# Five pairs of gate blocks in seven products instead of four: a hybrid attention block on one Trainium2 core

## The chip, the cores and the metric

The kernel runs on one core of a Trainium2 chip. The metric is the device time of one execution in microseconds (us): 1453.43 us is the median of three runs of the kernel before (1452.85 to 1456.15). The core has a matrix engine (PE, with its weight load PEld), a vector engine (DVE), a scalar engine (ACT), a general engine (POOL) and an engine (SP) that here does nothing but issue DMA transfers. Each engine works through its own queue in order and waits for the others by semaphores.

## The reference

One block of a streaming encoder on 1024 rows of width 1024, all in float32:

- `h = rms_norm(x)`, `proj = h @ w_in`. The last 2048 columns of `proj` go through a sigmoid and are the two gates, `gate_sb` and `gate_diff`. This document is about those 2048 columns; in blocks of 128 they are the sixteen gate blocks, 0 to 7 for the first gate and 8 to 15 for the second.
- stick-breaking attention, 8 heads of 64: strictly causal weights out of products of sigmoids
- differential attention, 4 heads of 2 x 64: the difference of two softmax maps with a position bias, then a norm per head
- `merged = gate_sb * (y_sb @ w_sb_out) + gate_diff * (y_diff @ w_diff_out)`, `x = x + rms_norm(merged @ w_o)`
- `u = relu(rms_norm(x) @ w_up) ** 2`, `x = x + rms_norm(u @ w_down)`

## The kernel before

**Precision.** A float32 factor is split into two parts that PE multiplies fast, `hi` (a cast by ACT) and `lo` (the rest, a subtraction by DVE). A product is three matmuls, hi x hi, hi x lo and lo x hi. A block of weights is loaded and split by `load_split` (L96 to L105).

**A gate block formed plainly.** `gate(b)` calls `project`: for each half of the 1024 rows of `h`, 8 slices of the depth times 3 matmuls of 128x512. That is 48 matmuls for a block. The result is copied out of the accumulator (L486) and stored to `gate_dram`; the sigmoid is taken when the merge reads it back.

**A pair of gate blocks in seven products.** A product of 2x2 blocks can be had from seven products instead of eight, if sums of the blocks are formed first. Here the four quarters of `h` (its depth and its rows halved) and the four quarters of two neighbouring gate blocks' weights are such blocks. One product of quarters (`product_h`, L541 to L550) is 4 x 3 = 12 matmuls, so a pair is 84 matmuls where two plain blocks are 96.

- `first_two(i)` forms two of the seven products, B11 and B21, for two pairs side by side. The first of them is kept in `p1_dram`, because it is needed again; the sum of both is a finished quarter of the gate.
- `last_products` forms the other five for all pairs, one pair after another. Before it can begin it takes four pages out of the SBUF slots with the tags `kh` and `kl`, loads the sums of `h` (`T1` to `T4`, formed in two earlier units by `form_sums`) and splits them (`split_sum`, L573 to L580).
- For each pair `pair_sums` (L590 to L596) loads both weight blocks and has POOL form four sums, and `split_pair` (L603, L604) splits them into `w24`, `w32` and `w1`. Then `start` runs the product with T2 (accumulator `g_b`), and the loop those with T3 and T4 (`g_d`) and T1 and B22 (`g_c`). Each product is followed by an addition on DVE (L631, L641, L645, L649, L653).

**The order of the work.** The attention runs in eight units: `u` = 0 to 3 for the stick-breaking heads, 4 to 7 for the differential heads. A unit's own steps alternate between PE (scores `z`, L273 and L274; transposes, L292; products with the values) and ACT, POOL and DVE. So each unit also has filler, work for PE that does not depend on the unit's chain: `fill(u)` first projects the next unit's queries, keys and values (`prepare(u + 1)`), then forms the gate blocks of `GATES[u]`, then, in unit 6, `first_two`, and in unit 7 `last_products`. `parts_of_fill(u)` counts the filler's parts, and the loop over the units hands them out in proportion to the work of the unit's steps (`while done * total < cost * size`). What is written is not the final order: a planner simulates the engines and gives each engine, at every point, the earliest written instruction that is ready. Later work, so also the next unit's filler, moves up into gaps where its slots and inputs allow.

Slots that matter below: two accumulators `acc`, two score banks `sc`, four slots `w` for split weights, two slots `raw` for loaded ones, four slots each for `kh`, `kl` and `qs` (two of a unit, two of the next), and a single slot for `bias`, which is loaded anew for each differential unit (L397) and patched by POOL (L400).

Before the change eight blocks are formed plainly, two each in units 0, 2, 4 and 7, and eight as four pairs:

```
PLAIN = 8
GATES = [range(0, 2), range(2, 2), range(2, 4), range(4, 4), range(4, 6), range(6, 6), range(6, 6), range(6, 8)]
```

Unit 6 has `first_two(0)` and `first_two(1)`; unit 7 has two plain blocks and then `last_products`.

After the units follow the merge (`half_mix`, L762), the output projection (L872) and the two MLP products (L994 and L1170), which the change does not touch.

Of the kernel before, what the change touches and what calls it, by code (L numbers as in the profile page):

```python
# [9 lines left out]
F32 = mybir.dt.float32  # L10
# [6 lines left out]
P = 128  # L17
# [4 lines left out]
HALF = 512  # L22
# [9 lines left out]
DFF = 4096  # L32
NF = DFF // P
ORDER = (3, 1, 2, 0)
PLAIN = 8
GATES = [range(0, 2), range(2, 2), range(2, 4), range(4, 4), range(4, 6), range(6, 6), range(6, 6), range(6, 8)]


SBQ, SBK, DFQ, DFK, GATE = 0, 4, 12, 16, 24
# [3 lines left out]
def hybrid_block_kernel(  # L43
# [23 lines left out]
    dram = ctx.enter_context(tc.tile_pool(name="dram", bufs=1, space=DRAM))  # L67
    ps = ctx.enter_context(tc.tile_pool(name="ps", bufs=1, space=PSUM))

    def acc_tile(name):  # L70
        return ps.tile([P, HALF], F32, tag="acc", name=name, bufs=2)
# [20 lines left out]
    def tmp_tile(name):  # L92
        return stream.tile([P, HALF], F32, tag="tmp", name=name, bufs=1)
# [45 lines left out]
        for name in ("A11", "A12", "A22", "S1", "S2", "S3", "S4")  # L139
    }  # L140
    t_dram = {name: [dram.tile([P, 2, HALF], F32, name=f"{name}_dram{q}") for q in range(2)] for name in ("T1", "T2", "T3", "T4")}
    p1_dram = dram.tile([4, P, HALF], F32, name="p1_dram")
    bias_dram = dram.tile([N_DIFF, NREL], F32, name="bias_dram")
    bias_rows = dram.tile([N_DIFF, P, NREL], F32, name="bias_rows")

# [9 lines left out]
    with ExitStack() as actx:  # L155
# [376 lines left out]
        def halves(w, i):  # L532
            return tuple(p[:, i * HALF:(i + 1) * HALF] for p in w)
# [20 lines left out]

        def first_two(i):

            bs = [PLAIN + 4 * i + 2 * e for e in range(2)]
            ws = [load_split(w_in[GATE + b], f"wa{b}") for b in bs]
            accs = [acc_tile(f"c11_{i}_{e}") for e in range(2)]
            for e in range(2):  # L560
                product_h(accs[e], halves(ws[e], 0), "B11")
                p1 = tmp_tile(f"p1_{i}_{e}")
                nc.scalar.copy(p1, accs[e])
                nc.sync.dma_start(out=p1_dram[2 * i + e], in_=p1)
                yield
            for e in range(2):
                product_h(accs[e], halves(ws[e], 1), "B21", first=False)
                gt = tmp_tile(f"gt_{bs[e]}_0")
                nc.any.tensor_copy(gt, accs[e])
                keep_gate(bs[e], 0, gt)  # L570
                yield
# [13 lines left out]
        def pair_sums(n):  # L585

            b = PLAIN + 2 * n
            f0, f1 = (stream.tile([P, S], F32, tag="raw", name=f"fw{n}_{i}") for i in range(2))
            for i, f in enumerate((f0, f1)):
                nc.sync.dma_start(out=f, in_=w_in[GATE + b + i])  # L590
            s1 = page_in["s1"][:, n % 2, :]
            a11, a12, a21, a22 = (f[:, i * HALF:(i + 1) * HALF] for f in (f0, f1) for i in range(2))
            nc.gpsimd.tensor_tensor(s1, a21, a22, op=ALU.add)
            nc.gpsimd.tensor_tensor(a21, a11, a21, op=ALU.subtract)
            nc.gpsimd.tensor_tensor(a11, s1, a11, op=ALU.subtract)
            nc.gpsimd.tensor_tensor(a12, a12, a11, op=ALU.subtract)  # L596
            return s1, f0, f1
# [11 lines left out]
        def last_products():  # L609

            for name, tag in (("v", "kh"), ("s1", "kh"), ("qu", "kl"), ("w1", "kl")):
                page_in[name] = pa.tile([P, 2, HALF], F32R if name == "w1" else F32, tag=tag, name=f"page_{name}", bufs=4)
            summed = pair_sums(0)
            for n in range(2):
                nc.sync.dma_start(out=page_in["v"][:, n, :], in_=p1_dram[n])
            split_sum("T2", sum_pages("T2"))
            t3_hi = pa.tile([P, 2, 2, HALF], F32R, tag="v", name="t3_hi", bufs=3)
            t3_lo = [pa.tile([P, 2, HALF], F32R, tag="qs", name=f"t3_lo{q}", bufs=4) for q in range(2)]
            split_sum("T3", [(t3_hi[:, q], t3_lo[q]) for q in range(2)])
            for name in ("T1", "T4"):  # L620
                split_sum(name, sum_pages(name))
            q, u21 = (page_in["qu"][:, e, :] for e in range(2))

            def start(n):
                nonlocal summed
                w1, w24, w32 = split_pair(n, *summed)
                summed = pair_sums(n + 1) if n < 3 else None
                b = acc_tile(f"g_b{n}")
                product_h(b, halves(w24, 0), "T2")
                v = page_in["v"][:, n % 2, :]  # L630
                nc.vector.tensor_tensor(v, b, v, op=ALU.add)  # L631
                return v, w1, w24, w32

            begun = start(0)
            yield
            for n in range(4):
                b0 = PLAIN + 2 * n
                v, w1, w24, w32 = begun
                d = acc_tile(f"g_d{n}")
                product_h(d, halves(w32, 0), "T3")  # L640
                nc.vector.tensor_tensor(q, d, v, op=ALU.add)  # L641
                yield
                c = acc_tile(f"g_c{n}")
                product_h(c, w1, "T1")
                nc.vector.tensor_tensor(q, c, q, op=ALU.add)  # L645
                keep_gate(b0 + 1, 1, q)
                yield
                product_h(d, halves(w32, 1), "T4", first=False)
                nc.vector.tensor_tensor(u21, d, v, op=ALU.add)  # L649
                keep_gate(b0 + 1, 0, u21)  # L650
                yield
                product_h(c, halves(w24, 1), "B22", first=False)
                nc.vector.tensor_tensor(v, c, v, op=ALU.add)  # L653
                keep_gate(b0, 1, v)
                if n < 2:
                    nc.sync.dma_start(out=v, in_=p1_dram[n + 2])
                yield
                if n < 3:
                    begun = start(n + 1)
                    yield  # L660

        n_units = N_SB + N_DIFF

        def fill(u):
            if u + 1 < n_units:
                yield from prepare(u + 1)
            for b in GATES[u]:
                yield from gate(b)
            if u == n_units - 2:
                for i in range(2):  # L670
                    yield from first_two(i)
            elif u == n_units - 1:
                yield from last_products()

        def parts_of_fill(u):
            n = 0 if u + 1 == n_units else 4 if u % 2 == 0 else 8
            return n + 2 * len(GATES[u]) + (0 if u < n_units - 2 else 8 if u == n_units - 2 else 20)


        xs = normalised(0)  # L680
# [283 lines left out]
    for t in range(NT):  # L964
# [19 lines left out]
        if t == 4:  # L984
            summed = sums(0, stream.tile([P, HALF], F32, tag="tmp", name="s1_0", bufs=1))
# [24 lines left out]
    for i in range(AHEAD // 2):  # L1010
        accs = [bank(BANKS[i % 2], f"c11_{2 * i + e}") for e in range(2)]
# [9 lines left out]
    summed = None  # L1021
# [215 lines left out]
    for left, other in zip(STORED, ("B11", "T1", "T2", "T4", "T3", "B22", "B21")):  # L1237
        accs = [bank(BANKS[t], f"d{left}_{t}") for t in range(4)]
# [63 lines left out]
```

## Time and profile before

| what | value |
|---|---|
| median of 3 runs | 1453.43 us |
| the profiled execution's own time | 1453.24 us |
| its span, first to last instruction | 1451.5 us |
| PE busy | 1425.8 us, 98% of the span |
| DVE, ACT, POOL busy | 1017.3, 751.4, 388.4 us |
| granted PE clock | 0.999 |

PE busy counts the time in which at least one matmul is under way; matmuls overlap, so it is not a sum of durations. A hole is a time in which PE has none. DVE, ACT and POOL times are sums of their instructions. The rows of the trace give for a group of instructions its engine, its source line, what it writes and reads, how often it runs, the total and the mean duration, and the idle time ahead of it with what ended that. In a table of stretches each engine has its busy time and, in brackets, its instruction count.

### The profile page before, as it was taken

Reading aid. Unit: us, or ns where it says so; the run is one execution under the profiler, and the core shown is the slowest. Engines: PE = TensorE matmul, PEld = TensorE weight load, DVE = VectorE, ACT = ScalarE, POOL = GpSimd, SP = SyncE. Lnnn points to the kernel's source line nnn. Section 1 sums busy time; section 2 is a strip of 40 time slices with the busy share of each in tenths; the row PEclk is TensorE's granted clock in tenths of the full one; section 3 lists DMA queues with packets and bytes.
Section 4 is the critical chain, followed back from the end, with each engine's and each line's share of the span. In section 5 each row is a group of like instructions: output and inputs, shape, how many; then the busy total and the mean of one; then the engine's idle time right before and its main releaser. Section 6 shows DMA issues by size and latency. Waiting matters only on the chain. (4 is left out here: it accounts for less than half of the span.)

```text
span 1451.5 us, 19994 instructions
## 1 busy us (share of the span) xinstructions
PE 1425.8 (98%) x7238; PEld 1209.1 (83%) x7238; DVE 1017.3 (70%) x1352; ACT 751.4 (52%) x1325; POOL 388.4 (27%) x377
## 2 busy tenths in 40 slices
PE   7999999999999999999999999999999999999997
PEld 6888998899889888788888878888888888888886
DVE  5477998788657777854755489766664669764783
ACT  6465665666656776444534465444444443534350
POOL 2012322234125002210002334333330357232611
PEclk9999999999999999999999999999999999999999
DMA  5432312222323247475657736544446785678681
GB/s 207 111 94 66 77 48 81 66 73 70 110 94 109 82 153 240 153 277 179 190 167 234 238 129 208 177 159 145 139 159 200 263 276 180 211 236 285 191 288 58
DMA packets 100283, 233.09 MB, mean 161 GB/s; under 512 B 9964, under 2 KB 25560, under 8 KB 100184
## 3 DMA queue, kind: packets, MB, share of 16 engines
q1 hardware_dynamic: 85784, 211.89, 46.2%
q10 hardware_dynamic: 14400, 19.93, 3.8%
q8 instruction: 57, 0.93, 0.3%
q14 instruction: 42, 0.34, 0.1%
HBM read 160.45 MB, written 65.29 MB: 156 GB/s over the span
## 5 line engine op out<-in xcount | busy, mean ns | idle before, releaser
L356 DVE TENSOR_TENSOR_SCAN rest<-rest 128x896 f32<-128x896 f32 (+3 forms) x64 | 88.1, 1385 | 16.4 <-POOL rest L351 15.6
L351 POOL TENSOR_SCALAR_AFFINE_SELECT rest<-rest 128x128 f32<-128x128 f32 x64 | 26.5, 414 | 242.4 <-ACT rest L347 242.4
L762 PE MATMUL mix<-y,wmix 128*128 128x512 f32 x384 | 88.2, 390 | 0.2 <-DMA y<-y_dram 0.2
L762 PEld LDWEIGHTS mix<-y,wmix 128*128 128x128 f32 x384 | 71.9, 188 | 15.4 <-DMA y<-y_dram 0.6
L824 DVE TENSOR_TENSOR lS_lo<-raw_S,lS_hi 128x1024 fp32r<-128x1024 f32 x32 | 53.9, 1683 | 40.1 <-ACT lS_hi L817 40.1
L1170 PE MATMUL dS<-rT_hi,lS_hi 128*128 128x512 f32 x192 | 74.7, 389 | 0.0
L1170 PE MATMUL dS<-rT_lo,lS_hi 128*128 128x512 f32 x192 | 74.7, 389 | 0.0
L1170 PE MATMUL dS<-rT_hi,lS_lo 128*128 128x512 f32 x192 | 74.7, 389 | 0.0
L817 ACT CAST lS_hi<-raw_S 128x1024 fp32r<-128x1024 f32 x32 | 33.6, 1051 | 74.5 <-DMA raw_S<-s_dramS 40.7
L419 ACT ACTIVATE s<-s,low 128x896 f32<-128x896 f32 (+7 forms) x64 | 49.7, 777 | 40.4 <-DVE low L414 40.0
L347 ACT ACTIVATE rest<-z 128x512 f32<-128x512 f32 (+2 forms) x96 | 48.1, 501 | 27.7 <-PE z L274 19.8
L299 DVE TENSOR_TENSOR wtl_sb<-tr_sb,wth_sb 128x512 fp32r<-128x512 f32 (+1 forms) x80 | 48.0, 628 | 8.5 <-ACT wth_sb L298 8.1
L298 ACT CAST wth_sb<-tr_sb 128x512 fp32r<-128x512 f32 (+1 forms) x80 | 41.2, 555 | 24.5 <-PE tr_sb L292 24.1
L351 POOL TENSOR_SCALAR_AFFINE_SELECT beta<-beta 128x128 f32<-128x128 f32 x64 | 52.2, 816 | 2.7 <-ACT beta L348 1.9
L414 DVE CUSTOM_DVE_ANT_0 s<-z,bias 128x512 f32<-128x512 f32 (+3 forms) x64 | 37.3, 586 | 21.1 <-PE z L274 14.9
L207 PE MATMUL acc_gate<-h,hi_gate 128*128 128x512 f32 x128 | 50.6, 396 | 0.0
L208 PE MATMUL acc_gate<-h,lo_gate 128*128 128x512 f32 x128 | 50.5, 394 | 0.0
L206 PE MATMUL acc_gate<-h,hi_gate 128*128 128x512 f32 x128 | 50.4, 394 | 0.0
L994 PE MATMUL c<-hB_lo,wa_hi 128*128 128x512 f32 x128 | 49.9, 390 | 0.0
L994 PE MATMUL c<-hB_hi,wa_hi 128*128 128x512 f32 x128 | 49.9, 390 | 0.0
L1170 PE MATMUL dA<-rB_hi,lA_hi 128*128 128x512 f32 x128 | 49.8, 389 | 0.0
L1170 PE MATMUL dA<-rB_lo,lA_hi 128*128 128x512 f32 x128 | 49.8, 389 | 0.0
(397 smaller groups left out, 4814.1 us busy)
## 6 DMA issues: line engine op xcount, KB each, us to landing
s_dramS<-us SPq DMA_DIRECT2D x64, 256.0 KB, 4.1
raw_S<-s_dramS SPq DMA_DIRECT2D x32, 512.0 KB, 4.1
s_dramA<-u ACTq DMA_DIRECT2D x48, 256.0 KB, 2.3
raw_A<-s_dramA SPq DMA_DIRECT2D x24, 512.0 KB, 4.3
y<-y_dram SPq DMA_DIRECT2D x16, 512.0 KB, 5.2
g<-gate_dram SPq DMA_DIRECT2D x16, 512.0 KB, 4.5
raw_up<-in_w_up_dram SPq DMA_DIRECT2D x16, 512.0 KB, 4.0
up<-in_w_up_dram SPq DMA_DIRECT2D x16, 512.0 KB, 4.0
```

The lines of the kernel that those rows point to most:

```text
L206: nc.tensor.matmul(acc, w_hi[:, ks], b_hi, start=(k == 0), stop=False)
L207: nc.tensor.matmul(acc, w_hi[:, ks], b_lo, start=False, stop=False)
L208: nc.tensor.matmul(acc, w_lo[:, ks], b_hi, start=False, stop=(k == NK - 1))
L299: nc.vector.tensor_tensor(lo[:, :n], tr[:, :n], f32(hi[:, :n]), op=ALU.subtract)
L347: nc.scalar.activation(rest[:, c0:c1], z, AF.Sigmoid, scale=-1.0)
L351: nc.gpsimd.affine_select(tl[:, dg], tl[:, dg], pattern=[[-1, P]], compare_op=ALU.is_gt, fill=fill, base=0, channel_multiplier=1,)
L356: nc.vector.tensor_tensor_scan(back, back, back, 1.0, op0=ALU.mult, op1=ALU.bypass)
L419: e = nc.scalar.activation(s[:, :nk], s[:, :nk], AF.Exp, bias=low, scale=-1.0, accum_out=sums[:, m:m + 1],)
L762: nc.tensor.matmul(accs[c], st, mv[:, cs], start=(first and k == 0), stop=(last and k == 3))
L824: nc.vector.tensor_tensor(lo, raw, f32(hi), op=ALU.subtract)
L994: nc.tensor.matmul(acc, st[:, ks], mv, start=(first and k == 0 and i == 0), stop=(k == 3 and i == 2), skip_group_check=True,)
L1170: nc.tensor.matmul(acc, st[:, e, ts], mv[:, e, :], start=(first and e == 0 and i == 0), stop=(last and e == 1 and i == 2))
```

## The change

Six blocks are formed plainly and ten as five pairs. The plain blocks stand in units 0, 2 (one each), 4 and 6 (two each), none in unit 7. All three calls of `first_two` are in unit 6, the third for a single pair. `last_products` runs over five pairs.

```diff
-PLAIN = 8
-GATES = [range(0, 2), range(2, 2), range(2, 4), range(4, 4), range(4, 6), range(6, 6), range(6, 6), range(6, 8)]
+PLAIN = 6
+PAIRS = (16 - PLAIN) // 2
+FIRST_TWO = (6, 6, 6)
+GATES = [range(0, 1), range(1, 1), range(1, 2), range(2, 2), range(2, 4), range(4, 4), range(4, 6), range(6, 6)]
...
-    p1_dram = dram.tile([4, P, HALF], F32, name="p1_dram")
+    p1_dram = dram.tile([PAIRS, P, HALF], F32, name="p1_dram")
...
         def first_two(i):
 
-            bs = [PLAIN + 4 * i + 2 * e for e in range(2)]
+            bs = [PLAIN + 2 * n for n in range(2 * i, min(2 * i + 2, PAIRS))]
             ws = [load_split(w_in[GATE + b], f"wa{b}") for b in bs]
-            accs = [acc_tile(f"c11_{i}_{e}") for e in range(2)]
-            for e in range(2):
+            accs = [acc_tile(f"c11_{i}_{e}") for e in range(len(bs))]
+            for e in range(len(bs)):
                 product_h(accs[e], halves(ws[e], 0), "B11")
                 p1 = tmp_tile(f"p1_{i}_{e}")
                 nc.scalar.copy(p1, accs[e])
                 nc.sync.dma_start(out=p1_dram[2 * i + e], in_=p1)
                 yield
-            for e in range(2):
+            for e in range(len(bs)):
                 product_h(accs[e], halves(ws[e], 1), "B21", first=False)
...
-                summed = pair_sums(n + 1) if n < 3 else None
+                summed = pair_sums(n + 1) if n < PAIRS - 1 else None
...
-            for n in range(4):
+            for n in range(PAIRS):
...
-                if n < 2:
+                if n < PAIRS - 2:
                     nc.sync.dma_start(out=v, in_=p1_dram[n + 2])
                 yield
-                if n < 3:
+                if n < PAIRS - 1:
                     begun = start(n + 1)
                     yield
...
             for b in GATES[u]:
                 yield from gate(b)
-            if u == n_units - 2:
-                for i in range(2):
+            for i, at in enumerate(FIRST_TWO):
+                if at == u:
                     yield from first_two(i)
-            elif u == n_units - 1:
+            if u == n_units - 1:
                 yield from last_products()
 
         def parts_of_fill(u):
             n = 0 if u + 1 == n_units else 4 if u % 2 == 0 else 8
-            return n + 2 * len(GATES[u]) + (0 if u < n_units - 2 else 8 if u == n_units - 2 else 20)
+            return n + 2 * len(GATES[u]) + 4 * FIRST_TWO.count(u) + (5 * PAIRS if u == n_units - 1 else 0)
```

## The prediction

> **What bounds the kernel now.** I read the page first, for the bound, then a table of stretches around the units that change, then the waits of PE in the one stretch where it has holes. The page:
>
> ```profile
> span 1451.5 us, 19994 instructions
> ```
>
> ```profile
> PE 1425.8 (98%) x7238; PEld 1209.1 (83%) x7238; DVE 1017.3 (70%) x1352; ACT 751.4 (52%) x1325; POOL 388.4 (27%) x377
> ...
> PEclk9999999999999999999999999999999999999999
> ```
>
> PE is covered for 98% of the span and its granted clock is full in every slice. "Busy" alone would not prove a bound, since matmuls overlap; the pace does. In the second MLP product, where nothing interrupts (the first fence below), 884 matmuls fill 200 us, 0.226 us each. The second fence has the stretches of units 0 to 3, then the end of unit 6 and unit 7 in pieces: the time of the two plain blocks (542:571), the first products of the pairs (571:600) and the rest.
>
> ```profile
> 1200.00:1400.00 200.00, 200.00 (x884) 165.58 (x884) 141.22 (x103) 85.98 (x102) 85.48 (x41) 1.00 0.72 232
> ```
>
> ```profile
> 66.00:142.00 76.00, 75.22 (x407) 64.49 (x406) 56.88 (x68) 43.14 (x90) 17.39 (x33) 1.00 0.37 101
> 142.00:209.00 67.00, 66.80 (x472) 62.01 (x470) 61.15 (x86) 45.07 (x105) 20.26 (x32) 1.00 0.23 59
> 209.00:283.00 74.00, 74.00 (x409) 63.97 (x408) 60.37 (x75) 43.61 (x91) 18.60 (x32) 1.00 0.26 77
> 283.00:351.00 68.00, 67.45 (x476) 62.61 (x475) 61.37 (x87) 46.59 (x105) 20.74 (x33) 1.00 0.23 60
> ...
> 542.00:571.00 29.00, 29.00 (x147) 24.55 (x146) 20.33 (x38) 17.70 (x37) 5.70 (x5) 1.00 0.77 251
> 571.00:600.00 29.00, 26.16 (x126) 21.01 (x125) 28.35 (x48) 20.93 (x36) 8.23 (x4) 1.00 0.47 150
> 600.00:647.00 47.00, 47.00 (x245) 39.93 (x244) 31.44 (x61) 20.95 (x43) 10.64 (x8) 1.00 0.67 225
> ```
>
> After the length come PE, PEld, DVE, ACT and POOL. Only one of these stretches has a hole worth naming: 571:600, where PE is covered 26.16 of 29 us (2.84 us of hole) and DVE is busy 28.35 of 29. There DVE sets the pace; everywhere else it is PE. What PE waited for in that stretch, longest first:
>
> ```profile
> PE z L273 <- DVE low L414: 1.0, 1, 1.0
> PE g_b L547 <- DVE page_qu L649: 0.9, 1, 0.9
> PE g_c L547 <- DVE page_qu L645: 0.6, 1, 0.6
> PE g_d L547 <- DVE T L580: 0.3, 1, 0.3
> ```
>
> All four end on DVE, 2.8 us together. So a matmul less is time won, unless the work that comes with it opens holes; unit 7 is where to look.
>
> **The change, part by part.** *Matmuls.* Before: 8 plain blocks x 48 + 4 pairs x 84 = 720. After: 6 x 48 + 5 x 84 = 708. Twelve less, at 0.226 us: **-2.7 us**, all on the bounding engine. By unit: units 0 and 2 lose 48 each (-10.9 us each); unit 6 gains 96 in plain blocks and 24 in the third call of `first_two` (+27.1 us); unit 7 loses 96 and gains 60 (-8.1 us).
>
> *Work beside PE.* Prices:
>
> ```profile
> L104 DVE TENSOR_TENSOR lo_gate<-raw_gate,hi_gate 128x1024 fp32r<-128x1024 f32 x8 | 9.8, 1231 | 0.5 <-ACT hi_gate L103 0.5
> L604 DVE TENSOR_TENSOR w_lo<-fw,w_hi 128x1024 fp32r<-128x1024 f32 x8 | 9.8, 1222 | 1.2 <-ACT w_hi L603 1.2
> L604 DVE TENSOR_TENSOR page_w<-page_s,page_w 128x512 fp32r<-128x512 f32 x4 | 4.3, 1072 | 3.1 <-ACT page_w L603 3.1
> L649 DVE TENSOR_TENSOR page_qu<-g_d,page_v 128x512 f32<-128x512 f32 x4 | 2.8, 689 | 4.1 <-PE g_d L547 4.1
> L603 ACT CAST w_hi<-fw 128x1024 fp32r<-128x1024 f32 x8 | 8.4, 1050 | 9.8 <-PE g_c L547 3.6 <-DMA gate_dram<-page_qu 3.5 <-issue 1.9
> L486 ACT COPY gt<-acc_gate 128x512 f32<-128x512 f32 x16 | 9.4, 588 | 4.9 <-PE acc_gate L208 2.6 <-issue 2.4
> L595 POOL TENSOR_TENSOR fw<-page_s,fw 128x512 f32<-128x512 f32 x4 | 6.4, 1610 | 0.3
> ```
>
> On DVE two plain blocks give back 2 x 1.23 = 2.5 us. A pair costs one split in `first_two` (1.23), two of `w24` and `w32` (2.44), one of `w1` (1.07) and five additions (3.45), 8.2 us: 5.7 us more. On ACT two plain blocks give back two casts and four copies (4.4 us); a pair costs three such casts, one of `w1` (taken as half, 0.5) and two copies, 4.8 us: nothing to speak of. POOL gets four more sums, about 6.4 us by L595. The DMA queue of SP gets one store and one load of `p1_dram` more and loads the two weight blocks once more. Cover: behind 571:600, DVE is busy 31.44 of 47 us and POOL 10.64, so a fifth round fits there at no cost. If the cover were gone, as in 571:600, it costs up to 5.7 us of DVE.
>
> *Units 0 to 3.* Without the one block, unit 0 is 76 - 10.9 = 65.1 us for DVE work of 56.88 - 1.2, a load of 86%; unit 2 is 63.1 us for 59.2, 94%. Units 1 and 3 already run at 91% and 90% with holes of 0.20 and 0.55 us. I take **+0.3 us**; between 0 (the planner finds the gaps) and 1.5 us (twice the holes of the odd units).
>
> *The start of unit 7.* Here the cover goes. The last scores of unit 6, the reload of the bias, the first POOL sums and their repetition in the next pair:
>
> ```profile
> 544.87 0.28 PE L273 MATMUL z<-kh_dfk,qs_dfq 128*128 128x256 f32 x1
> ...
> 548.29 1.03 SPq L397 DMA_DIRECT2D bias<-bias_rows  x1
> 550.66 1.29 POOL L593 TENSOR_TENSOR page_s<-fw 128x512 f32<-128x512 f32 x1 [63.24 <-DMA t_lo<-T_dram]
> ...
> 555.10 1.34 POOL L596 TENSOR_TENSOR fw<-fw 128x512 f32<-128x512 f32 x1
> ...
> 571.69 0.61 PE L547 MATMUL g_b<-T,w_hi 128*128 128x512 f32 x2
> ...
> 577.01 2.22 POOL L593 TENSOR_TENSOR page_s<-fw 128x512 f32<-128x512 f32 x1 [19.64 <-DVE low L414]
> ...
> 583.87 1.60 POOL L596 TENSOR_TENSOR fw<-fw 128x512 f32<-128x512 f32 x1
> ```
>
> And the four transfers of the bias, from issue to landing:
>
> ```profile
> DMA to landing us min/median/max: 5.6/8.2/8.8
> ```
>
> The pages of `last_products` need the `kh` and `kl` slots of unit 6, so its chain begins with that unit's last score: four sums on POOL (550.66 to 556.44: 5.8 us; the second pair's took 577.01 to 585.47: 8.5), a cast (1.05) and a split (1.22), then `g_b`. That is 8.1 to 10.8 us. Unit 7's own scores wait as long, because the single bias slot is reloaded first: 5.6 to 8.8 us. Before, two plain blocks that need neither fill this time:
>
> ```profile
> 542.00:571.00 29.00, 24.23 (x95) 17.18 (x95) 1.74 (x3) 1.00 0.77 251
> ```
>
> This row is the 542:571 stretch for the plain blocks' accumulator alone: 95 of PE's 147 matmuls there, 95 x 0.226 = 21.5 of 29 us. The other 52 (unit 6's last transposes and products, unit 7's first scores) took 7.5 us. After the change only these are left against a chain of 8.1 to 10.8, and `parts_of_fill` sharpens it: it counts 4 + 4 + 12 = 20 parts for unit 6, but the third `first_two` yields 2, not 4, so 18 exist and they are all handed out before unit 6's last step. A chain of 8.1 to 10.8 us against 7.5 us leaves 0.6 to 3.3 us, and the 7.5 us are themselves a chain over ACT and DVE. I take **+2.5 us** of hole; at the low end 0, if the planner runs unit 6's last scores in earlier gaps so that the chain starts sooner; at the high end 8.1, if all of that PE work has run before the chain begins.
>
> The Trainium skill, "SBUF — State Buffer", section "Who interferes with whom", says a DVE instruction with two SBUF inputs and a POOL instruction that reads SBUF lock each other out for a whole instruction. The rows agree: 1.29 us for L593 when DVE was half idle, 2.22 when it was full. By that rule the long chain of 10.8 us would hold whenever DVE is splitting at that time, and the sum would be 0.8 us higher, at a hole of 3.3 us.
>
> *The holes of 571:600.* DVE was full there because the splits of T1 to T4 (L580) fell together with the first two pairs' splits and unit 7's first softmax:
>
> ```profile
> L580 DVE TENSOR_TENSOR T<-T,T 128x1024 fp32r<-128x1024 f32 x6 | 8.3, 1389 | 0.2 <-ACT T L577 0.2
> L580 DVE TENSOR_TENSOR t_lo<-t_lo,t_hi 128x1024 fp32r<-128x1024 f32 x2 | 2.4, 1222 | 0.2 <-ACT t_hi L577 0.2
> ```
>
> Eight splits, 10.7 us. Their slots are the pages of `h` that plain blocks and `first_two` read; these now finish in unit 6, so the splits can run in the boundary's waiting time or, for T2, earlier. I take **-1.0 us** of the 2.84; between -2.8 (all gone) and +2 (a third of the 5.7 us that DVE gains in work).
>
> *Sum*, against the profiled execution's 1453.24 us (span 1451.5 plus 1.7 around it): -2.7 + 0.3 + 2.5 - 1.0 = -0.9, so 1452.3. The median of the runs is 0.2 above the profiled one, so **1452.5 us**.
>
> **The rivals.**
> - *All cover stays* (faster). Unit 6's last scores run early, the boundary closes, and the T splits clear out of 571:600: -2.7 - 2.8 = -5.5, 1447.9 us; with holes as before it is -2.7, 1450.7. For it: the planner left just 2.84 us of hole in 60 us of unit 7. Against it: in the kernel before every unit still had filler when the next began.
> - *The start of unit 7 runs dry* (slower). One mechanism, the chain from unit 6's last score to `g_b` with no filler: at the full 8.1 us hole the sum is -2.7 + 0.3 + 8.1 - 1.0 = +4.7, 1458.1 us. It decides from a hole of 5.6 us on (5.6 - 2.7 = 2.9). For it: both ways forward, sums and bias, wait for the same last score. Against it: 7.5 us of PE work is there to fill.
> - *DVE becomes the bound of unit 7* (slower): if 28.35 of 29 goes on through the unit, the added 5.7 us all show, -2.7 + 5.7 = +3.0, 1456.4 us. Against it: 31.44 of 47 us.
> - *A slower pace after the hole* (slower): in this trace the granted clock is 1.00 in every stretch. If a hole of 8.1 us let it fall to half for one product, twelve matmuls would take 2.7 us more, 1460.8 us. The Trainium skill, "TensorE: Matmul & The Clock Gate", Part 1, says that an idle window of about 3.4 us does halve the clock; no hole in these stretches is that long, so no row here tests it.
>
> **How the numbers follow.** A measurement of this kernel tells about 0.2%, 2.9 us, from no change. The forecast, within 2.9 us of before (1450.5 to 1456.3), has 0.50; all cover staying, as far as it goes beyond 2.9 us, 0.28; the dry start 0.13; DVE as the bound 0.06; the slower pace 0.03. So faster 0.28, same 0.50, slower 0.22. The likeliest case's own range is 1450.5 to 1456.3. For 8 in 10 it reaches down to 1447.5 (no holes at all) and up to 1458 (the dry start at its full price).
>
> **What would show it.** The PE count falls by 12. In units 0 and 2 the distance from first score to first score shrinks by about 11 us with no new waits on DVE. Right for the boundary: one or two holes of 0.6 to 3.3 us in all between unit 6's last score and the first `g_b`, released by DVE's split (L604) or the scores' DVE. Right for the T splits: L580 before the first `g_b`, and fewer than 2.8 us of waits in the 29 us behind it. The forecast is wrong if holes at the boundary sum to under 0.5 or over 5.6 us, if waits of PE on DVE appear in units 1 to 3, or if holes turn up where the change does nothing, in the merge or the MLP.

## The result, and the profile after

The kernel after takes **1467.14 us** (median of five runs, 1464.84 to 1469.30) against 1453.43: a ratio of 1.0086, 95% interval 1.0074 to 1.0098. By that ratio it is slower by 12.5 us (0.0086 x 1453.4; the two medians are 13.7 us apart), where 1452.5 was forecast and 1458 was the upper end of the range. The profiled execution took 1464.84 us.

The page of the kernel after, its span and busy times:

```profile
span 1463.1 us, 20015 instructions
...
PE 1428.4 (98%) x7226; PEld 1209.6 (83%) x7226; DVE 1027.2 (70%) x1359; ACT 755.0 (52%) x1325; POOL 388.2 (27%) x381
```

PE has the 12 matmuls less that were counted, and is "98%" as before. Where the time was lost the page does not show; it has to be found by stage. The distances below run from the first scores (or the first matmul of a stage) to the next such matmul, in the two profiled executions; the third column is the matmuls that a stage gained or lost, at 0.226 us.

| stage | before | after | matmuls alone | beyond them |
|---|---|---|---|---|
| units 0 to 3 | 284.8 | 269.4 | -21.7 | **+6.3** |
| units 4 and 5 | 135.0 | 134.7 | 0 | -0.3 |
| units 6 and 7 | 160.5 | 184.3 | +19.0 | **+4.8** |
| merge | 88.7 | 88.3 | 0 | -0.4 |
| output projection | 92.5 | 95.5 | 0 | **+3.0** |
| from the up product to the end | 623.5 | 624.3 | 0 | +0.8 |

The last column sums to 14.2; less 2.7 it is, but for rounding, the 11.6 us between the two spans. Three places lost time.

**Units 0 to 3.** The stretches of the kernel after, each one unit long (length, then PE, PEld, DVE, ACT, POOL with counts, clock, DMA):

```profile
66.00:133.00 67.00, 66.50 (x362) 56.98 (x360) 51.87 (x60) 40.51 (x85) 15.86 (x29) 1.00 0.35 98
133.00:202.00 69.00, 66.14 (x470) 61.30 (x471) 64.02 (x94) 45.84 (x108) 19.97 (x36) 1.00 0.21 58
202.00:269.00 67.00, 65.50 (x364) 56.54 (x363) 57.15 (x70) 41.54 (x87) 16.05 (x30) 1.00 0.28 76
269.00:336.00 67.00, 66.02 (x472) 61.16 (x471) 63.11 (x94) 46.74 (x107) 18.82 (x35) 1.00 0.21 52
```

Units 0 and 2 became shorter, but unit 1 has a hole of 2.86 us (69.00 - 66.14) where it had 0.20, units 2 and 3 of 1.5 and 1.0. What PE waited for between 66 and 352 us, kernel after (total, times, longest):

```profile
PE av L328 <- DVE wtl_sb L301: 2.6, 3, 1.5
PE z L275 <- ACT beta L350: 1.6, 3, 1.0
PE acc_sbv L256 <- DVE kl_sbk L238: 0.8, 1, 0.8
PE acc_sbk L208 <- DVE qs_sbq L223: 0.5, 1, 0.5
PE acc_sbv L257 <- DVE lo_sbv L106: 0.3, 1, 0.3
```

and the same list of the kernel before:

```profile
PE acc_sbk L206 <- DVE qs_sbq L221: 0.8, 1, 0.8
PE av L326 <- DVE wtl_sb L299: 0.4, 1, 0.4
```

5.8 us for 1.2. DVE is busy 64.02 of 69.00 and 63.11 of 67.00 us in units 1 and 3, 93 and 94%, where it had 91 and 90. PE's longest waits are for DVE's splits of the unit's own attention weights (`wtl_sb`). The waits are not the whole loss: PE's holes grew from 1.5 to 5.8 us, 4.3 of the 6.3; the other 2 us are in time in which PE counts as covered.

**The boundary of units 6 and 7.** The timeline of the kernel after, PE's rows (start, duration; in brackets the idle time before and what ended it):

```profile
550.87 0.28 PE L276 MATMUL z<-kl_dfk,qs_dfq 128*128 128x256 f32 x1
554.32 1.54 PE L294 MATMUL tr_df<-ident,s 128*128 128x128 f32 x6 [3.18 <-DVE s L434]
555.52 1.20 PE L549 MATMUL c<-h,hi_wa 128*128 128x512 f32 x2
...
560.20 0.39 PE L549 MATMUL c<-h,lo_wa 128*128 128x512 f32 x1
```

DVE and POOL at that time:

```profile
551.23 1.10 DVE L390 SCALAR_TENSOR_TENSOR sq<-sq,r 128x512 f32<-128x512 f32 x1
552.25 2.01 DVE L434 SCALAR_TENSOR_TENSOR s<-s,sums,s 128x768 f32<-128x768 f32 x1
...
551.86 1.59 POOL L596 TENSOR_TENSOR fw<-fw,fw 128x512 f32<-128x512 f32 x1
```

and the same time cut into stretches of 3.41 us, the last figure but two being the granted clock:

```profile
549.74:553.16 3.42, 1.30 (x8) 0.86 (x6) 2.83 (x5) 2.00 (x6) 2.57 (x2) 1.00 0.87 283
553.16:556.57 3.41, 2.25 (x9) 2.06 (x10) 3.41 (x4) 2.80 (x5) 3.25 (x3) 0.50 0.89 320
556.57:559.98 3.41, 3.41 (x10) 2.65 (x9) 3.41 (x6) 3.12 (x6) 0.53 (x1) 0.50 0.81 304
559.98:563.40 3.42, 3.42 (x23) 2.87 (x22) 3.42 (x7) 3.42 (x7) 0.00 (x0) 1.00 0.67 208
```

There is one hole of 3.2 us (3.3 with a gap of 0.1 just ahead of it), and behind it the clock is 0.50 for 6.83 us: the third row has ten matmuls where 3.41 / 0.226 = 15 would fit. The twelve matmuls of the third `first_two`'s second product take 0.41 us each. An estimate: at half clock 2.25 + 3.41 us of matmuls are up to 2.8 us longer than they need be (the twelve alone are 2.2), so the hole costs nearly twice its length. Later unit 7 is better than before: its holes sum to 1.0 us, where they were 2.8.

Two ways forward were shut at once. The transposes wait for DVE's `s`. The twelve matmuls wait for ACT's copy of the product before them, and on ACT that copy stands behind a cast of `T` that waits for its load:

```profile
553.08 1.04 ACT L579 CAST T<-T 128x1024 fp32r<-128x1024 f32 x1 [1.39 <-DMA T<-T_dram]
554.03 0.61 ACT L605 CAST page_w<-page_s 128x512 fp32r<-128x512 f32 x1
554.55 0.58 ACT L565 COPY p<-c 128x512 f32<-128x512 f32 x1
```

**The output projection.** One of ACT's mean squares there, what PE waited for, and what ACT waited for on that store, all between 735 and 840 us of the kernel after:

```profile
794.81 0.60 ACT L111 ACTIVATE or<-o 128x512 f32<-128x512 f32 x1 [3.32 <-DMA x_dram<-xr]
```

```profile
PE trh L900 <- ACT ht L906: 2.2, 1, 2.2
...
ACT or L111 <- DMA x_dram<-xr: 7.7, 2, 4.4
```

and the last of these in the kernel before:

```profile
ACT or L109 <- DMA x_dram<-xr: 2.7, 1, 2.7
```

One row tile of `o` gets an SBUF slot out of which a row of `x` is still being stored; the mean square waits for that store, ACT's copies (`ht`) are queued behind it, and PE's next transposes wait for these.

### The profile page after: what moved, and what is told of

Same layout as the page of the kernel before. It is cut to its first block, busy times and chain, and to the rows that moved or that the text cites. A ratio compares the mean times of both kernels' runs of the same rounds, so it can differ in the third digit from the quotient of the medians.

```text
span 1463.1 us, 20015 instructions
## 1 busy us (share of the span) xinstructions
PE 1428.4 (98%) x7226; PEld 1209.6 (83%) x7226; DVE 1027.2 (70%) x1359; ACT 755.0 (52%) x1325; POOL 388.2 (27%) x381
## 5 line engine op out<-in xcount | busy, mean ns | idle before, releaser
L826 DVE TENSOR_TENSOR lA_lo<-raw_A,lA_hi 128x1024 fp32r<-128x1024 f32 x24 | 36.0, 1500 | 20.0 <-ACT lA_hi L819 18.5
L1172 PE MATMUL dA<-rB_hi,lA_lo 128*128 128x512 f32 x128 | 49.8, 389 | 0.0
L996 PE MATMUL c<-hB_hi,wa_lo 128*128 128x512 f32 x128 | 49.7, 389 | 0.0
L359 DVE TENSOR_TENSOR beta<-beta,rest 128x895 f32<-128x895 f32 (+3 forms) x64 | 48.2, 758 | 1.9
```

What stands on the lines that cost most here:

```text
L359: nc.vector.tensor_tensor(beta[:, :nk - 1], beta[:, :nk - 1], rest[:, 1:nk], op=ALU.mult)
L826: nc.vector.tensor_tensor(lo, raw, f32(hi), op=ALU.subtract)
L996: nc.tensor.matmul(acc, st[:, ks], mv, start=(first and k == 0 and i == 0), stop=(k == 3 and i == 2), skip_group_check=True,)
L1172: nc.tensor.matmul(acc, st[:, e, ts], mv[:, e, :], start=(first and e == 0 and i == 0), stop=(last and e == 1 and i == 2))
```

## The experiments

The first theory took up the first two of these readings: **A**, the plain blocks of units 0 to 3 were cover for a DVE that has no time left; **B**, the plain blocks of unit 7 were cover for the chain from unit 6 to the first sums; and the change removed both kinds. All times below are medians; a ratio is against the kernel before on the same chip in the same stretch of runs (its medians were 1454.7 to 1455.5 there). "The gates" are the number of plain blocks per unit; after, it is 1, 0, 1, 0, 2, 0, 2, 0, and `FIRST_TWO = (6, 6, 6)`.

### e1 and e2: one half of the change each

e1 is the kernel after with the plain blocks of units 0 to 3 left where they were, so that unit 6 loses its two:

```
-GATES: 1, 0, 1, 0, 2, 0, 2, 0
+GATES: 2, 0, 2, 0, 2, 0, 0, 0
```

> Five pairs as in the changed kernel, but the six plain blocks stand two each in units 0, 2 and 4, none in unit 6; first_two stays three times in unit 6. Theory A (units 0 to 3 became bound by DVE when units 0 and 2 lost a block each, which cost 6.5 us against the matmuls taken out): units 0 to 3 go back to 284.8 us as before, the holes of the boundary of units 6 and 7 stay, total about 1460.6 us. Theory B (the whole loss comes from the boundary of units 6 and 7, where cover is missing): unit 6 has two blocks of cover less still, so no gain, 1467 us or more.

e2 is the kernel before, four pairs, with only its plain blocks moved:

```
-GATES: 2, 0, 2, 0, 2, 0, 0, 2
+GATES: 1, 0, 1, 0, 2, 0, 2, 2
```

> Four pairs and eight plain blocks as before; alone the move of one block each out of units 0 and 2 into unit 6 is made (plain blocks 1, 0, 1, 0, 2, 0, 2, 2). No matmul less, unit 7 keeps its two plain blocks. Theory A: about +6.5 us over before, 1460 us, with PE waiting for DVE and ACT in units 1 to 3. Theory B: nothing lost there, 1453.4 us within 2 us.

e1: 1462.86 us, ratio 1.0053 (1.0035 to 1.0070). Units 0 to 3 take 284.5 us, so A's loss is gone; but units 6 and 7 take 167.0 where their matmuls and the old holes give 157.8, with a hole of 5.0 us and 10.2 us at half clock. e2: 1463.98 us, ratio 1.0060 (1.0043 to 1.0077): moving two blocks, without one matmul more or less, costs 8.5 us, and no hole opens between units 6 and 7. In its profile units 0 to 3 are 8.3 us over what their matmuls give; 6.8 us at half clock are part of that. The two halves are separate losses; each alone is more than the 2.7 us that the twelve matmuls are worth.

### e3 and e4: the third `first_two` elsewhere

```
-FIRST_TWO = (6, 6, 6)
+FIRST_TWO = (6, 6, 4)
```

e3 does this to the kernel after, e4 to e1.

> The changed kernel with the third call of first_two, the one for a single pair, in unit 4 instead of last in unit 6. Theory C (the 3.3 us hole at the end of unit 6 is the chain product, copy, product of the single pair, whose copy waits for the one slot tmp): that hole goes, about 1463.8 us. Theory B (it is missing cover): 24 matmuls less of cover in unit 6, hole as long or longer, 1467 us or more.

> Both: plain blocks two each in units 0, 2 and 4, the single pair's first_two in unit 4. Theories A and C together: 1467.1 - 6.5 - 3.3 = 1457.3 us; 1454 us if the 3.3 us that the changed kernel also lost behind the attention (a hole in the output projection) go too. Theory B: unit 6 has the least filler of all, the boundary opens to 5 us or more, 1462 us or more.

e3: 1471.06 us, ratio 1.0100 (1.0079 to 1.0122); e4: 1466.86, 1.0079 (1.0062 to 1.0097). With the call in unit 4, e4 is 4.0 us slower than e1, on the same chip. e3 is not clearly slower than the kernel after (their ratios differ by 2.0 us and their intervals overlap), and not faster by either figure. The boundary has holes of 2.1, 0.8 and 1.8 us (e3), with half clock for 10.2 and 13.7 us. So it is not the third call's place in unit 6 that opens the boundary.

### e5: the two blocks back in unit 7

The kernel after with its blocks placed anew: two each in units 0 and 2 as before the change, one in unit 4, and one in unit 7, before `last_products`:

```
-GATES: 1, 0, 1, 0, 2, 0, 2, 0
+GATES: 2, 0, 2, 0, 1, 0, 0, 1
```

> Five pairs, plain blocks 2, 0, 2, 0, 1, 0, 0, 1 over units 0 to 7: units 0 and 2 keep both blocks, the two blocks that the fifth pair replaces come out of unit 4 and out of unit 7, which keeps one as cover. first_two three times in unit 6. Theory A+B (the 14 us are units 0 to 3 that cannot be shortened, and a boundary of units 6 and 7 without cover): both causes are gone, the 12 matmuls show, 1450.7 to 1453 us where before is 1453.4. Theory D (any block taken out of an attention unit shows only about 7.5 of its 10.9 us, unit 4 too): 1454 to 1457 us.

1467.15 us, ratio 1.0083 (1.0059 to 1.0108). Units 4 and 5 take 133.9 us where 48 matmuls less should give 124.1: a block taken out of unit 4 gains 1.1 us of its 10.9, in a profile with 6.8 us at half clock there. In e8 below, with the same blocks and no half clock there, the two units take 131.3, a gain of 3.7. PE's longest waits in 335 to 475 us are of the same kind as in units 0 to 3, now in the differential heads:

```profile
PE av_d L371 <- DVE wtl_df L301: 1.7, 1, 1.7
PE acc_dfv L257 <- DVE lo_dfv L106: 1.0, 1, 1.0
PE z L275 <- DVE low L416: 0.6, 1, 0.6
```

But DVE, third after the length, had room in unit 4, the first of these two stretches:

```profile
351.00:426.00 75.00, 71.99 (x362) 60.40 (x361) 47.98 (x107) 41.13 (x81) 21.56 (x25) 0.95 0.35 104
426.00:485.00 59.00, 56.98 (x384) 51.46 (x383) 45.80 (x107) 38.96 (x85) 24.51 (x23) 1.00 0.32 92
```

So a block can be cover where DVE is busy 64% of the time. PE's longest wait there ends at 416.88 us, on DVE work that comes in a bunch: DVE had stood idle for 2.6 us, until 410.56, and was then busy almost without a pause. There is no slack in unit 4 to pay for unit 7's cover. At the boundary the one block in unit 7 did help in this run: no hole there is over 0.5 us.

### e6: is it DVE's throughput?

The kernel after with 14 of DVE's splits in units 0 to 3 left out: for these weights (two gate blocks, queries, keys and values) `hi` is used in place of `lo`. The low part of these products is therefore left out of the result. The edit also takes no `w` slot for these `lo` parts, so it frees slots as well as DVE time.

```
         nc.scalar.copy(hi, raw)
+        if name in RELIEVED:
+            return hi, hi
         nc.vector.tensor_tensor(lo, raw, f32(hi), op=ALU.subtract)
```

> The changed kernel without 14 of DVE's weight splits (1.22 us each, 17 us) that run in units 0 to 3; the matmuls use the hi part in place of the lo part there, so their number and order of dependence on the attention stay, and the lo part of these weights is left out of the result. Theory A (DVE's throughput bounds units 1 to 3): PE's 5.8 us of waits in 66 to 352 us shrink to about the 1.2 us of before, 1462 us. Rival (the waits are the chain's latency over ACT, POOL and DVE, which has too little PE filler beside it): waits and time stay, 1467 us.

1461.64 us, ratio 1.0047 (1.0032 to 1.0062): 5.5 us less than the kernel after. Units 0 to 3 take 265.6 us for 269.4, and PE's waits there fall from 5.8 to 3.0 us:

```profile
PE av L331 <- DVE wtl_sb L304: 2.1, 5, 0.9
PE z L278 <- ACT beta L353: 0.7, 2, 0.3
PE acc_dfk L211 <- DVE qs_dfq L226: 0.2, 1, 0.2
```

PE's holes there fall from 5.8 to 3.3 us, so the work that was left out has a part in them. But the time was not won. Units 4 and 5 take 137.5 us for 134.7, units 6 and 7 185.5 for 184.3: from the first scores to the merge both kernels take 588.5 us. Eight matmuls less fall into units 0 to 3, eleven more into units 4 and 5, and PE waits there instead, between 332 and 472 us of e6:

```profile
PE acc_dfv L260 <- DVE lo_dfv L109: 1.1, 1, 1.1
PE tr_df L297 <- DVE s L437: 0.8, 1, 0.8
PE av_d L373 <- ACT wth_df L303: 0.3, 1, 0.3
```

The boundary's hole stayed at 3.2 us. What e6 is shorter by in its profile lies behind the units: the output projection takes 92.5 us for 95.5, and the merge is 0.5 shorter. So A is not shown: DVE's splits take part in the waits of units 0 to 3, but whether DVE's load or the length of the units' chains sets the loss stays open, as e5 does for unit 4.

### e7 and e8: POOL's sums earlier

Two pages of `last_products` are taken from a free slot of the values' kind, and `T3`'s `hi` pages go to `kh` in exchange, so that POOL need not wait for unit 6's `kh`; e7 on the kernel after, e8 on e5.

```
-for name, tag in (("v", "kh"), ("s1", "kh"), ("qu", "kl"), ("w1", "kl")):
+sv = pa.tile([P, 2, 2, HALF], F32, tag="v", name="page_sv", bufs=3)
+page_in["s1"], page_in["v"] = sv[:, 0], sv[:, 1]
...
```

> The changed kernel with the pages for the first sums and p1 in the third slot v, which is free in unit 6, and T3's hi pages in kh in exchange: POOL can form the first pair's sums before unit 6's last score. Theory E (the 3.3 us hole at the end of unit 6 is DVE held up by POOL's sums: its instructions of 0.7 to 1.2 us take 1.7 to 2.3 there): the hole shrinks to under 1 us, 1464 us. Theory B (missing cover): PE has no more to do than before, the hole stays or moves, 1467 us.

> Both e5 and e7. If the boundary in e5 still has a hole from POOL's sums, it closes: 1450 to 1451 us, faster than before by about 3 us. If the cover of one plain block already closes it: as e5 within 1 us.

1466.50 us, ratio 1.0088 (1.0066 to 1.0110), and 1466.42, 1.0079 (1.0055 to 1.0103): no difference to the versions without it. In e7 POOL's first sum started at 550.75 us, as before the edit (550.51), now held by the load of its weights. The edit did not move what it was to move, so e7 says nothing on the theory; e14 asks the question in another way. In e8 the sums did move, from 552.83 us (e5) to 545.61. The boundary did not close: a hole of 3.1 us opened, this time ahead of unit 7's scores, and no half clock followed it:

```profile
555.14 0.50 PE L275 MATMUL z<-kh_dfk,qs_dfq 128*128 128x512 f32 x1 [3.08 <-DVE low L416]
```

### e9 and e10: cover for the boundary

e9 is e1 with the third `first_two` in unit 7, ahead of `last_products`. e10 is the kernel after, and forms plain block 5 a second time in unit 7: 48 matmuls, 10.9 us of PE work that nobody needs.

```
-FIRST_TWO = (6, 6, 6)
+FIRST_TWO = (6, 6, 7)     # e9, with GATES 2, 0, 2, 0, 2, 0, 0, 0
-range(6, 6)]
+range(5, 6)]              # e10, the last entry of GATES
```

> Five pairs, plain blocks two each in units 0, 2 and 4 as in e1, but the single pair's first_two (24 matmuls, 5.4 us, that wait for none of unit 6's slots) at the start of unit 7 as cover for the chain to the first g_b. Theory F (a hole of PE at the boundary costs twice: its own length, and after it PE runs at half the granted clock for 3.4 us or a multiple, as the traces so far show): with the hole under about 1.5 us the clock stays and the 12 matmuls show for a part, 1452 to 1456 us. Rival (the single pair's own chain product, copy, product opens the hole wherever it stands without a partner): 1460 us or more, with a stretch at half clock.

> The changed kernel with 48 matmuls more: plain block 5 is formed a second time in unit 7, ahead of the five products. Its work is 10.9 us of PE. Theory F with B (missing cover): hole of 3.3 us and 6.8 us at half clock go, so the block costs only about 10.9 - 3.3 - 3.4 = 4 us over the changed kernel, or less. Rival (the boundary is no matter of cover): the full 10.9 us, 1478 us.

> The changed kernel again, on one chip with the others. If the 3.3 us that it lost behind the attention (first merge matmul to the end: 808.1 us against 804.7 before) come from the change, that stretch is again 3 us longer than in the repeat of the kernel before; if they are scatter of the transfers there, the two stretches differ otherwise or not at all.

e11, the kernel after again on that chip: 1467.73 us, ratio 1.0094 (1.0077 to 1.0111), with the same holes. e9: 1459.43, 1.0029 (1.0017 to 1.0040); against e1, units 6 and 7 take 164.4 us for 167.0, and the longest hole of the boundary is 1.5 us for 5.0. e10: 1472.68, 1.0138 (1.0115 to 1.0161): the useless block costs 5.0 us over e11, not 10.9. Not all of that is the boundary. In the profiles units 6 and 7 take 192.0 us in e10 for 184.4 in e11, 7.6 more, and the output projection 92.5 for 96.8. So 3.3 of the 10.9 us fill time that PE otherwise stands or runs at half clock; the rest of the difference is the third loss, which e10 does not have. The hole behind unit 6's scores and the half clock are gone, but the block brings a hole of its own:

```profile
PE acc_gate L208 <- ACT gt L571: 2.6, 1, 2.6
```

This is B: cover in unit 7 takes away part of the boundary's loss, in e9 and in e10.

### e12: the kernel before again

> The kernel before again: the stretch from the first merge matmul to the end, 804.7 us in its first profile, for comparison with e11, and whether its granted clock again never drops inside.

1452.47 us in its one execution; the stages from the merge on take 804.5 us, where the first profile had 804.7, and 808.1 and 808.9 in the two profiles of the kernel after. The 3 us of the output projection are no accident of one profile, though 3.4 us at half clock are part of it in e11.

### e13 and e14: what the hole is made of

In e9 PE stood from 511.3 to 513.3 us for a copy on ACT, since T2's casts ran ahead of it on ACT:

```profile
PE c L549 <- ACT p L565: 3.2, 2, 2.1
PE g_b L549 <- ACT w_hi L605: 1.5, 1, 1.5
PE tr_df L294 <- DVE s L434: 1.4, 1, 1.4
```

e13 is e9 with these casts behind the last such copy (`last_p1` lists the copies); e14 is the kernel after without POOL's sums for the first pair, so that its gate blocks 6 and 7 are not those of the reference.

```
-if name != "T2":                                   # e13
-    after(cast, freed[-1])
+after(cast, freed[-1] if name != "T2" else last_p1[-1])
...
+if n == 0:                                         # e14, in pair_sums
+    nc.gpsimd.memset(s1, 0.0)
+    return s1, f0, f1
```

> The version with the plain blocks left in units 0, 2 and 4 and the third first_two in unit 7 (1459.43 us, 4.2 us over before), with T2's two casts on ACT held behind the last copy of a first product (p1). In that version T2's casts run ahead of a cast and a p1 copy, and PE stands from 510.9 to 513.3 us until the copy comes. Theory F (that order is the cause of that hole): the hole goes, the time is 1456.5 to 1457.8, still over before, because the boundary holes of 0.7 to 1.7 us and the half clock behind them stay. Rival G (the unit has no filler, whatever the order): the hole only moves, T2's splits are late for the first g_b, and the time is 1459 to 1463.

> The kernel after, with POOL's four sums for the first pair left out (its weights then enter unsummed, a zero page takes the place of the first sum; the gate blocks 6 and 7 are not those of the reference). Theory E (POOL's sums and DVE's instructions slow each other in the boundary of units 6 and 7, where DVE's additions take 1.1 to 2.3 us for 0.7 to 1.2): the hole of 3.3 us at 551 falls to 1 us or less, the half clock behind it goes, units 6 and 7 take 178 to 180 us for 184.3, and the time is 1461 to 1463. Rival (the hole is the scores' own chain over the bias, DVE and ACT, whatever POOL does): the hole stays at 2.5 us or more with a half clock behind it, and the time is 1466 to 1468.

e13: 1456.71 us, ratio 1.0018 (1.0006 to 1.0031), as theory F has it: the hole at 511 us is gone. Its profiled execution, 1463.26 us, is the longest of ten and has 98.0 us in the output projection, so its late stages are not read. e14: 1464.40 us, ratio 1.0064 (1.0043 to 1.0086), between the two expectations. The hole at the boundary falls from 3.2 to 1.6 us and there is no half clock behind it; units 6 and 7 take 182.1 us for 184.3. DVE's instructions that took 1.10 and 2.01 us beside POOL are short now:

```profile
555.61 0.69 DVE L390 SCALAR_TENSOR_TENSOR sq<-sq,r 128x512 f32<-128x512 f32 x1
556.33 1.02 DVE L434 SCALAR_TENSOR_TENSOR s<-s,sums,s 128x768 f32<-128x768 f32 x1
```

What is left of the hole is the wait for ACT's copy of the third first product, so about half of it was POOL's doing. That is not all contention: DVE's two instructions are 0.41 and 0.99 us shorter, 1.4 of the 3.2 us, but without the sums the first `g_b` also starts at 555.36 us, before the hole, and its twelve matmuls are cover. PE's waits in 545 to 585 us:

```profile
PE c L549 <- ACT p L565: 1.6, 1, 1.6
PE g_b L549 <- ACT w_hi L608: 1.1, 1, 1.1
```

### e15 and e16: the slots of the output projection

The four row slots are handed out as two kinds of two in turn, so that rows of `x` and of `o` never share one; e15 in the kernel after, e16 in the one before.

```
 def row(name, shape=None):
-    return pb.tile(shape or [P, S], F32, tag="row", name=name, bufs=4)
+    rows[0] += 1
+    return pb.tile(shape or [P, S], F32, tag=f"row{rows[0] % 2}", name=name, bufs=2)
```

> The kernel after, with the four row slots of the part behind the merge divided into two kinds of two, handed out in turn, so that in the output projection the rows of x and the rows of o never share a slot. Theory H (the 3.0 us that the output projection lost come from a mean square that has to write into a slot whose store is still under way): its waits on that store go, the distance from the first matmul of the output projection to the first of the up product is 92.5 us again for 95.5, and the time is 1463.5 to 1465. Rival (the loss comes from what stands before it, such as the time at which weights land): the distance stays at 95 or more, and so does the time, 1466.5 to 1468.

> The kernel before, with the same division of the row slots. It is what the division costs by itself. By theory H nothing, since the output projection already takes 92.5 us there: 1453 to 1454.5. If the division starves later stages of slots (the up product's loads), both this kernel and the divided kernel after lose the same: over 1455.

e15: 1463.92 us, ratio 1.0066 (1.0049 to 1.0082). ACT's list of waits has no row for that store any more, the output projection takes 93.0 us, and the kernel about 3 us less than the one after. e16: 1453.52, ratio 0.9998 (0.9989 to 1.0007): before, the division is worth nothing. Theory H holds: the third loss is the planner's assignment of slots, which came out differently in the changed kernel. The other profiles agree. Where ACT waits for that store twice, 7.7 to 9.4 us in all, the output projection takes 94.8 to 99.4 us (the kernel after, e5, e7, e8, e11, e13); where it waits once, 2.5 to 2.7 us, it takes 92.5 (before, e1, e2, e4, e6, e9, e10, e12); e3 and e14 lie between, with 5.7 and 3.4 us of waits and 92.6 and 93.4 us. A difference between two versions can hold 3 us of this.

### e17 and e18: everything taken back

e17 is e13 with e15's division. e18 has in addition the third `first_two`'s first product in a free slot in place of the single slot `tmp`.

```
+if i < 2:
     p1 = tmp_tile(f"p1_{i}_{e}")
+else:
+    p1 = pa.tile([P, 2, 2, HALF], F32, tag="v", name="p1_last", bufs=3)[:, 0, 0, :]
```

> Five pairs with all that the runs showed: the plain blocks left in units 0, 2 and 4, the third first_two in unit 7, T2's casts behind the last p1 copy, and the row slots in two kinds. Theory (the losses add up and can be taken back one by one): the version without the two kinds took 1456.7 us, 1.0018 of before, with 98.0 us in the output projection of its profile; with 92.5 to 93 there it gains 1 to 4 us, 1452.5 to 1455.5, a ratio of 0.998 to 1.001. Rival (the planner gives the gain back elsewhere): 1456 or more, a ratio of 1.0015 or more.

> As the one before, and the third first_two's first product goes through a free slot of the values' kind and not through the single tmp slot. In the profile without this, its finished quarter waits 2.35 us on ACT for that slot's store, and the cast of w_hi and with it g_b wait behind it (PE stands 1.5 us at 553.7 to 555.3, half clock follows). Theory (the single slot makes the second of the two boundary holes): that hole goes, and 0.5 to 2.5 us with it, a ratio of 0.997 to 1.0. Rival (the boundary is short of filler, and what is taken from one wait goes into the next): no difference beyond 0.5 us.

e17: 1455.85 us, ratio 1.0011 (1.0002 to 1.0020); e18: 1455.97, ratio 1.0006 (0.9997 to 1.0014), where the kernel before had 1455.12. e17 lies between its theory (up to 1455.5) and its rival (from 1456 on). The single slot was not what held the boundary (e18's rival). With four edits five pairs are as fast as four, and not faster: units 0 to 5 and the late stages are as in the kernel before, and units 6 and 7 take 162.5 us in e18, where 160.5 less 2.7 would be 157.8. PE's waits at the boundary in e18, between 545 and 562 us:

```profile
PE g_b L549 <- DVE w_lo L608: 1.7, 1, 1.7
PE av_d L371 <- DVE wtl_df L301: 1.7, 1, 1.7
PE g_b L549 <- ACT w_hi L607: 0.3, 1, 0.3
```

One wait is the unit's own chain (`av_d`), two are the pair's (`g_b`). No version with five pairs beat the kernel before.

## Why the prediction was wrong

- *Twelve matmuls less, -2.7 us.* Right in the count. Nothing of it was left over.
- *Units 0 to 3, +0.3, at most 1.5.* This is the step that failed most: **+6.3 us**. The loads of 86 and 94% were means over a whole unit, and were taken as room, and each unit's DVE work was taken to stay in it. In the stretches of the odd units PE has the matmuls it had (470 and 472 for 472 and 476), but DVE has 94 instructions in each for 86 and 87, and 64.02 and 63.11 us for 61.15 and 61.37: work that the longer even units had held now falls there (68 and 75 instructions in these before, 60 and 70 after). Unit 1's hole went from 0.20 to 2.86 us. e1 takes the term back, and e2 shows it nearly alone (8.5 us for the whole kernel). That DVE's instructions are what PE waits for is shown; that DVE's load, and not the chain's length, sets the size is not (e5, e6). The test that the prediction gave itself, waits of PE on DVE in units 1 to 3, is what came.
- *The start of unit 7, +2.5 us.* Right in place and size: 3.2 us, released by the scores' DVE, and from POOL's first sum to the first `g_b` (550.51 to 561.02 us) it is 10.5 us, near the long chain of 10.8. The match with its 3.3 us is in part luck: the hole ends on unit 6's own transposes, and the filler that was counted on stood behind ACT's copy. Its price was wrong. The halved clock behind it adds up to 2.8 us.
- *The slower pace after the hole.* It was given 0.03, since it was tied to a hole of 8.1 us and one product. A hole of 3.2 us was enough. The condition was mistaken, the mechanism was not (last section).
- *The holes of 571:600, -1.0 us.* The sign was right and the size too small: the holes of unit 7 after the boundary went from 2.8 to 1.0 us. With the hole and the halved clock this gives 3.3 + 2.8 - 1.8 = 4.3 of the 4.8 us measured in units 6 and 7.
- *DVE as the bound of unit 7.* Did not come; PE's new waits on DVE are in units 1 to 3 and at the boundary.
- *Nothing behind the units.* The sum had no term for it. Wrong by 3.0 us: the change does nothing in the output projection, but a list of instructions that is planned anew gets other slots.
- *The fifth pair's extra DVE work* was not taken apart from the rest by any run.

## What to carry to other kernels

A filler that can run anywhere costs its length only where the bounding engine has nothing else to wait for: here a block of 10.9 us gave back 7.7 us out of units 0 and 2 (15.4 for two), 1.1 to 3.7 out of unit 4, and one put into unit 7 for nothing cost 7.6 there. So before saving or moving such work, ask of each stage what the filler covers: which chain over the other engines runs beside it, and how long PE would stand without it. Neither "98% busy", true before and after, nor the second engine's mean load (64% in unit 4) answers that. A saving of 2.7 us is less than one hole, and a planned order can lose as much again far from the edit.

## What the runs showed of the hardware

**The clock goes by windows, not by holes.** In every profile with more than one of them the stretches at half clock begin a whole number of 3.413 us apart (in e2 at 139.3, 272.4, 671.8 and 869.8 us: 39, 117 and 58 windows). Cutting each profile into these windows, from unit 0 to the last matmul, and taking those at full clock by how much of them PE was covered (matmuls' ends are modelled):

| PE covered | windows | half clock in the next |
|---|---|---|
| under 45% | 18 | 18 |
| 45 to 62% | 37 | 15 |
| over 62% | about 8000 | 0 |

The Trainium skill, "TensorE: Matmul & The Clock Gate", Part 1, has such free-running windows and ties half clock to an idle one. The runs agree on the windows, but none has to be idle: under 45% covered was always enough, 45 to 62% sometimes, and a hole's cost depends on how it falls on the windows, which begin elsewhere in every run. In e2 0.33 and 1.48 us of hole within one window were followed by a window at half clock; in e10 a hole of 2.6 us was not, as two windows shared it, nor was the 3.1 us of e8. The stretches of e2, then of e10:

```profile
135.00:139.00 4.00, 2.19 (x14) 1.41 (x12) 3.94 (x6) 3.93 (x11) 1.95 (x4) 1.00 0.38 100
139.30:142.70 3.40, 3.40 (x18) 3.21 (x16) 3.28 (x8) 1.85 (x4) 0.88 (x2) 0.50 0.06 22
```

```profile
559.70:563.10 3.40, 2.33 (x14) 1.74 (x12) 3.29 (x8) 3.40 (x9) 0.82 (x1) 1.00 0.73 167
563.10:566.50 3.40, 1.88 (x8) 1.57 (x9) 2.69 (x3) 2.84 (x6) 0.14 (x1) 1.00 0.92 314
```

It goes with part of the spread of the runs of one kernel: of the five of the kernel after, those with a mean clock of 0.996 took 1464.8 and 1466.2 us, those with 0.994 took 1467.1 and twice 1469.3. One window at half clock is, as an estimate, 0.5 x 3.41 = 1.7 us, or 0.0012 of the mean. It is not all of the spread: two runs of e5 at 0.997 took 1463.5 and 1470.9 us.

**POOL and DVE slow each other.** DVE's instructions of 0.69 and 1.02 us in e14 took 1.10 and 2.01 us in the kernel after beside POOL's sums, and a split 2.31 us for 1.22. The Trainium skill, "SBUF — State Buffer", section "Who interferes with whom", has this as a lock on a shared pair of ports; the runs agree in direction. In the kernel after, these two instructions were 1.4 us longer ahead of a hole of 3.2.
